# Interleaved RoPE on one core: a longer fp32 head on two queues, its result stored early, and longer VectorE steps

## Chip, cores, metric

The kernel runs on one core of a Trainium2 chip. The metric is the device time of one execution in microseconds (us), as a median over runs. Times inside an execution are counted from the start of the profile's span. The span of a profiled run is about 1.8 us shorter than its device time (before: 316.0 against 317.78). "The packet records" below are the trace's single DMA packets, with their start, length, queue and size.

## The reference

```python
# x: (8, 2048, 16, 64) fp32; cos, sin: (2048, 32) fp32
x_pairs = x.reshape(batch, seq_len, num_heads, head_dim // 2, 2)
x1, x2 = x_pairs[..., 0], x_pairs[..., 1]
out1 = x1 * cos - x2 * sin        # cos, sin broadcast over batch and heads
out2 = x1 * sin + x2 * cos
out = np.stack([out1, out2], axis=-1).reshape(batch, seq_len, num_heads, head_dim)
```

The input is 67.1 MB of fp32 and the output as much. There are three vector passes per element, and nothing for TensorE.

## The kernel before

Each of the 128 partitions holds 16 consecutive positions (`K = 16`) of each of the 8 batches, 1024 values a position. A batch is loaded by GpSimd's software queue, which casts fp32 to bf16 on the way, is rotated in place by VectorE in steps of `KP` positions, and is stored by the same queue, cast back to fp32. Five batch buffers (`NX = 5`) exist, so five loads are queued at once at the start, and load 5 needs the buffer that store 0 frees. Two small exceptions use fp32 and the SP queue, which does not cast: the first `HEAD = 2` positions of batch 0 come in early, and the last `TAIL = 4` positions of batch 7 go out from a buffer that ScalarE has cast.

```python
KP = 4; NX = 5; HEAD = 2; TAIL = 4
def load(b, k0=0):                       # ... allocate tiles[b], bf16
    nc.gpsimd.dma_start(out=tiles[b][:, k0:], in_=x_t[b, :, k0:])
def store(b, k1=K):
    nc.gpsimd.dma_start(out=out_t[b, :, :k1], in_=tiles[b][:, :k1])
def rotate(b, k0, k1):
    # ... three VectorE passes over positions k0..k1:
    # qt = xp * s_tab ; xp = xp * c_tab ; xp = xp + qt with each pair swapped

head = stage.tile([P, TAIL, HD], fp32, name="st")
for k in range(HEAD):
    nc.sync.dma_start(out=head[:, k : k + 1], in_=x_t[0, :, k : k + 1])
nc.sync.dma_start(out=cos_sb, in_=cos_t)
nc.sync.dma_start(out=sin_sb, in_=sin_t)
load(0, HEAD)
for b in range(1, NX):
    load(b)
nc.scalar.copy(out=tiles[0][:, :HEAD], in_=head[:, :HEAD])
# ... VectorE builds the bf16 tables s_tab, c_tab from sin_sb, cos_sb
for b in range(B):
    if b == 0:
        rotate(b, 0, HEAD)
        rotate(b, HEAD, KP)
    for k0 in range(KP if b == 0 else 0, K, KP):
        rotate(b, k0, k0 + KP)
    if b < B - 1:
        store(b)
    if b >= 1 and b - 1 + NX < B:
        load(b - 1 + NX)
store(B - 1, K - TAIL)
# ... ScalarE casts the last TAIL positions to fp32, the SP queue stores them
```

## Time and profile before

| | before |
|---|---|
| time, median of the runs beside the changed kernel | 317.45 us (317.34 to 317.79, 6 runs) |
| VectorE busy, first to last | 221.8 us, from 44.2 to 269 us |
| first packet to last packet of the DMA engines | 1.74 to 314.8 us |
| first and second store issued | 74.5 and 102.2 us |

From the page of the kernel before: the span, the busy times, the rows of 40 slices (tenths busy), the queues (packets, MB, share of the time of 16 engines) and the HBM traffic.

```profile
span 316.0 us, 198 instructions
...
DVE 221.8 (70%) x102; ACT 6.9 (2%) x4; POOL 8.9 (3%) x20
...
DVE  0000039999999999999999999999999999100000
...
DMA  9899999999999999999999999999999999999996
...
q0 software_dynamic: 2304, 98.04, 96.8%
q1 hardware_dynamic: 720, 3.67, 3.1%
...
HBM read 67.63 MB, written 67.11 MB: 426 GB/s over the span
```

VectorE (DVE) is idle for the first five slices and the last five, while the DMA row is at 9 throughout. The two queues' shares add up to the whole span. The Trainium skill ("DMA: Bandwidth & Descriptors", "Specifications") gives 435 GB/s as the ceiling of the fabric. The 426 GB/s over the whole span, start and end included, are 98% of that. A second limit on that page, about 358 GB/s of HBM per core (a stack's bandwidth divided by the two cores that share it), is not what this trace shows; here one core runs.

The timeline of the kernel before: start, duration, engine, line and operation, and in brackets the idle time ahead of it and what ended that. SPq is the issue of a DMA on the SP queue; a POOL line with `DMA_DIRECT2D` is an issue on the software queue.

```profile
0.74 0.85 SPq L85 DMA_DIRECT2D st<-in_x_dram  x2
1.24 2.80 POOL L56 DMA_DIRECT2D xt<-in_x_dram  x5 [0.80 <-PEq L144]
1.64 0.42 SPq L86 DMA_DIRECT2D cos_sb<-in_cos_dram  x1
2.11 0.43 SPq L87 DMA_DIRECT2D sin_sb<-in_sin_dram  x1
6.36 1.28 ACT L92 ACT_TABLE_LOAD   x1 [6.36 <-DMA st<-in_x_dram]
...
44.22 0.45 DVE L94 CAST s_tab<-sin_sb 128x512 bf16<-128x512 f32 x1 [44.22 <-DMA sin_sb<-in_sin_dram]
...
74.53 0.54 POOL L59 DMA_DIRECT2D out_dram<-xt  x1 [70.48 <-DVE xt L80]
...
102.17 0.54 POOL L59 DMA_DIRECT2D out_dram<-xt  x1 [27.11 <-DVE xt L80]
...
121.79 0.54 POOL L56 DMA_DIRECT2D xt<-in_x_dram  x1 [19.08 <-DMA out_dram<-xt]
```

Two things are to be seen. The sine table, 256 KB issued at 2.1 us, lands only at 44.2 us. And both first stores are queued before the engines need them. The trace's records of single packets show the last queued load ending at 101.8 us and the second store's data starting at 120.6 us, directly behind the first's. A packet of the software queue is one partition's 64 KB of fp32 and occupies an engine for 2.437 us (load) or 2.447 us (store).

### The profile page before, as it was taken

Reading aid. Unit: us, or ns where it says so; the run is one execution under the profiler, and the core shown is the slowest. Engines: PE = TensorE matmul, PEld = TensorE weight load, DVE = VectorE, ACT = ScalarE, POOL = GpSimd, SP = SyncE. Lnnn points to the kernel's source line nnn. Section 1 sums busy time; section 2 is a strip of 40 time slices with the busy share of each in tenths; the row PEclk is TensorE's granted clock in tenths of the full one; section 3 lists DMA queues with packets and bytes.
Section 4 is the critical chain, followed back from the end, with each engine's and each line's share of the span. In section 5 each row is a group of like instructions: output and inputs, shape, how many; then the busy total and the mean of one; then the engine's idle time right before and its main releaser. Section 6 shows DMA issues by size and latency. Waiting matters only on the chain.

```text
span 316.0 us, 198 instructions
## 1 busy us (share of the span) xinstructions
DVE 221.8 (70%) x102; ACT 6.9 (2%) x4; POOL 8.9 (3%) x20
## 2 busy tenths in 40 slices
DVE  0000039999999999999999999999999999100000
ACT  1200000000000000000000000000000000000400
POOL 3000000000000000000000000000000000000000
DMA  9899999999999999999999999999999999999996
GB/s 241 198 257 212 212 207 236 228 199 199 253 212 265 398 498 431 398 332 261 203 399 465 328 203 199 481 448 265 199 307 423 398 440 481 406 398 481 417 431 263
DMA packets 3025, 101.72 MB, mean 322 GB/s; under 512 B 336, under 2 KB 336, under 8 KB 848
## 3 DMA queue, kind: packets, MB, share of 16 engines
q0 software_dynamic: 2304, 98.04, 96.8%
q1 hardware_dynamic: 720, 3.67, 3.1%
q14 instruction: 1, 0.01, 0.0%
HBM read 67.63 MB, written 67.11 MB: 426 GB/s over the span
## 4 chain that ended last, share of the span: by engine, by line
another core or an unknown queue 91%; DMA 2%; ACTq 1%; ACT 1%; SPq 0%; issue 0%
DMA st<-in_x_dram 2%; ACTq L144 1%; ACT xt L92 1%; ACT L92 0%; SPq L85 0%; ACT xt L116 0%; ACTq L116 0%; ACTq L92 0%
## 5 line engine op out<-in xcount | busy, mean ns | idle before, releaser
L75 DVE TENSOR_TENSOR xt<-xt,c_tab 128x4096 bf16<-128x4096 bf16 (+1 forms) x33 | 73.5, 2228 | 1.1
L80 DVE TENSOR_TENSOR xt<-xt,qt 128x4096 bf16<-128x4096 bf16 (+1 forms) x33 | 73.5, 2228 | 1.1
L74 DVE TENSOR_TENSOR qt<-xt,s_tab 128x4096 bf16<-128x4096 bf16 (+1 forms) x33 | 73.5, 2228 | 1.1
L94 DVE CAST s_tab<-sin_sb 128x512 bf16<-128x512 f32 x1 | 0.5, 453 | 44.2 <-DMA sin_sb<-in_sin_dram 44.2
L59 POOL DMA_DIRECT2D out_dram<-xt x8 | 4.3, 535 | 202.1 <-DVE xt L80 202.1
L116 ACT COPY xt<-xt 1x1 bf16<-1x1 bf16 x1 | 0.2, 193 | 286.3 <-DMA out_dram<-xt 286.3
L56 POOL DMA_DIRECT2D xt<-in_x_dram x8 | 4.4, 561 | 52.1 <-DMA out_dram<-xt 51.3
L117 ACT CAST st<-xt 128x4096 f32<-128x4096 bf16 x1 | 3.6, 3599 | 0.0
L92 ACT CAST xt<-st 128x2048 bf16<-128x2048 f32 x1 | 1.9, 1899 | 0.0
L92 ACT ACT_TABLE_LOAD x1 | 1.3, 1283 | 6.4 <-DMA st<-in_x_dram 6.4
L96 DVE CAST c_tab<-cos_sb 128x1024 bf16<-128x1024 f32 x1 | 0.7, 684 | 0.0
L95 DVE TENSOR_SCALAR s_tab<-sin_sb 128x512 bf16<-128x512 f32 x1 | 0.4, 443 | 0.0
L133 POOL MEMSET const-float32-0.0<- 128x1 f32 x1 | 0.1, 99 | 0.2 <-issue 0.2
L133 POOL MEMSET const-bfloat16-1.0<- 128x1 bf16 x1 | 0.1, 102 | 0.0
L133 POOL MEMSET const-float32-1.0<- 128x1 f32 x1 | 0.1, 99 | 0.0
L133 POOL MEMSET const-uint8-127<- 128x1 uint8 x1 | 0.1, 99 | 0.0
## 6 DMA issues: line engine op xcount, KB each, us to landing
xt<-in_x_dram POOLq DMA_DIRECT2D x7, 4096.0 KB, 58.0
out_dram<-xt POOLq DMA_DIRECT2D x1, 6144.0 KB, 49.4
xt<-in_x_dram POOLq DMA_DIRECT2D x1, 3584.0 KB, 22.7
out_dram<-st SPq DMA_DIRECT2D x1, 2048.0 KB, 15.5
st<-in_x_dram SPq DMA_DIRECT2D x2, 512.0 KB, 4.5
cos_sb<-in_cos_dram SPq DMA_DIRECT2D x1, 256.0 KB, 22.4
sin_sb<-in_sin_dram SPq DMA_DIRECT2D x1, 256.0 KB, 42.1
out_dram<-xt POOLq DMA_DIRECT2D x7, 54.0
```

Of the source, the lines that this page charges most:

```text
L56: nc.gpsimd.dma_start(out=tiles[b][:, k0:], in_=x_t[b, :, k0:])
L59: nc.gpsimd.dma_start(out=out_t[b, :, :k1], in_=tiles[b][:, :k1])
L74: nc.vector.tensor_tensor(out=rows(qt[:, :nk]), in0=rows(xp), in1=tab(s_tab), op=mult)
L75: nc.vector.tensor_tensor(out=rows(xp), in0=rows(xp), in1=tab(c_tab), op=mult)
L80: nc.vector.tensor_tensor(out=x3, in0=x3, in1=q_swap, op=add)
L92: nc.scalar.copy(out=tiles[0][:, :HEAD], in_=head[:, :HEAD])
L94: nc.vector.tensor_copy(out=s2[:, :, 0], in_=sin_sb)
L95: nc.vector.tensor_scalar_mul(s2[:, :, 1], sin_sb, -1.0)
L96: nc.vector.tensor_copy(out=c_tab.rearrange("p k (i j) -> p (k i) j", j=2), in_=cos_sb.to_broadcast([P, K * D2, 2]),)
L117: nc.scalar.copy(out=tail, in_=tiles[B - 1][:, K - TAIL :])
L133: nc = _bacc.Bacc("TRN2", target_bir_lowering=False, num_devices=1)
L144: with _tile.TileContext(nc) as tc:
```

## The change

Its intent seems to be to start the vector work earlier and to use the engines better. Four head positions instead of two come in fp32, one DMA each, in turn on the SP and the Activation queue, and each queue brings one table. The rotated head goes back out early in fp32 on the SP queue. VectorE works in steps of 8 positions, which halves its instructions.

```diff
-    KP = 4
+    KP = 8
-    HEAD = 2
+    HEAD = 4
+    HEAD_RUNS = [(0, 1), (1, 2), (2, 4)]
...
-    def store(b, k1=K):
-        nc.gpsimd.dma_start(out=out_t[b, :, :k1], in_=tiles[b][:, :k1])
+    def store(b, k0=0, k1=K):
+        nc.gpsimd.dma_start(out=out_t[b, :, k0:k1], in_=tiles[b][:, k0:k1])
...
         for k in range(HEAD):
-            nc.sync.dma_start(out=head[:, k : k + 1], in_=x_t[0, :, k : k + 1])
+            q = (nc.sync, nc.scalar)[k % 2]
+            q.dma_start(out=head[:, k : k + 1], in_=x_t[0, :, k : k + 1])
         nc.sync.dma_start(out=cos_sb, in_=cos_t)
-        nc.sync.dma_start(out=sin_sb, in_=sin_t)
+        nc.scalar.dma_start(out=sin_sb, in_=sin_t)
...
                 rotate(b, 0, HEAD)
+                nc.scalar.copy(out=head, in_=tiles[b][:, :HEAD])
+                for k0, k1 in HEAD_RUNS:
+                    nc.sync.dma_start(out=out_t[b, :, k0:k1], in_=head[:, k0:k1])
                 rotate(b, HEAD, KP)
...
-                store(b)
+                store(b, HEAD if b == 0 else 0)
```

More of the change, by code (lines that the diff above doesn't have):

```diff
@@ L82 @@
     with tc.manual_schedule():
-        head = stage.tile([P, TAIL, HD], fp32, name="st")
+        head = stage.tile([P, HEAD, HD], fp32, name="st")
         for k in range(HEAD):
-            nc.sync.dma_start(out=head[:, k : k + 1], in_=x_t[0, :, k : k + 1])
+            q = (nc.sync, nc.scalar)[k % 2]
+            q.dma_start(out=head[:, k : k + 1], in_=x_t[0, :, k : k + 1])
         nc.sync.dma_start(out=cos_sb, in_=cos_t)
-        nc.sync.dma_start(out=sin_sb, in_=sin_t)
+        nc.scalar.dma_start(out=sin_sb, in_=sin_t)
         load(0, HEAD)
@@ L90 @@
             load(b)
-        nc.scalar.copy(out=tiles[0][:, :HEAD], in_=head[:, :HEAD])
+        nc.scalar.copy(out=tiles[0][:, :HEAD], in_=head)
         s2 = s_tab.rearrange("p k (i j) -> p (k i) j", j=2)
@@ L106 @@
             if b < B - 1:
-                store(b)
+                store(b, HEAD if b == 0 else 0)
             if b >= 1 and b - 1 + NX < B:
                 load(b - 1 + NX)
-        store(B - 1, K - TAIL)
+        store(B - 1, 0, K - TAIL)
         tail = stage.tile([P, TAIL, HD], fp32, name="st")
```

## The prediction

> **What bounds the kernel now.** The 16 DMA engines. The page's slice row shows DMA at 9 tenths or more in nearly all 40 slices (8 in the second, 6 in the last), VectorE 70% busy, ScalarE 2%. The queue part gives the software queue 96.8% and the hardware queue 3.1% of the engines' time. The trace's records of single packets sharpen this: from 4 to 312 us all 16 engines have a packet; only 0 to 4 us (first packet at 1.74, share 0.46) and 312 to 316 us (share 0.52) are not full. VectorE starts at 44.2 us, when the sine table lands (view of waits), ends at 269 and never stops for a load. The timeline shows the first store issued at 74.5 us, the second at 102, while the five loads queued at the start keep the engines busy until about 101. No idle DMA time is there to fill.
>
> A packet costs by its fp32 side, either way: load of 64 KB 2.437 us, store of 64 KB 2.447, 56 KB 2.129, 48 KB 1.84, 16 KB 0.611, 4 KB 0.159 (0.165 with the gap after it), table row of 2 KB 0.096.
>
> **The change, costed.**
> - Head: 2 MB instead of 1 in fp32 rows of 4 KB. Per engine 16 more packets x 0.165 = 2.6 us; the first cast load shrinks from 56 to 48 KB: 8 x 0.29 = 2.3. Net +0.3 us.
> - Early result: 16 packets of 4 KB and 8 of 8 KB (estimate 16 x 0.165 + 8 x 0.31 = 5.1 us); first store 48 instead of 64 KB: 8 x 0.6 = 4.8. Net +0.3 us.
> - Two issuing queues: an issue takes 0.42 us. First data can't come before 1.74 us; overlapped slow first packets (0.5 to 1 us) may return 0.2 to 0.5. The Trainium skill ("DMA: Bandwidth & Descriptors", "Issuing engines are not separate DMA queues") says queues share the 16 engines and save issue time only; the trace agrees so far as one queue fills all 16.
> - VectorE by 8: a pass takes 1.25 us for 2048 elements, 2.33 for 4096, so 0.17 fixed; 48 fewer save 8 us of VectorE, none on the critical path.
> - ScalarE: one more 3.6 us cast, off the path.
>
> **When compute starts.** The same page ("Queues, rings and completion order") has engines take turns between queues by packet. The trace agrees: cos landed 22.4 us after issue, its 8 packets per engine each behind a 2.13 us packet of the first load; sin behind the second load. After the change the last two head pieces either stay early or go behind the first load, so the tables land near 24 or near 44 us. I lean to 44 (0.6). Either way the first two stores are queued before 101 and 120 us, so the engines don't run dry.
>
> **Predicted time.** +0.6 us of packets, -0.3 at the start: 317.6 us; 8 in 10 within 316.2 to 318.8. Faster by over 2%: 0.02; within 2%: 0.96; slower: 0.02.
>
> **What would show it.** DMA slices at 9 throughout; hardware queue's share near 6%, software's near 94%; VectorE busy near 214 us; first store of tile 0 before 75 us; tail unchanged: last cast near 296 us, last store issued near 300.
>
> **What would make it wrong.** Small fp32 stores between loads costing far more than 0.16 us, or overlapping them in an engine (read of one with write of the other); tables landing after 65 us, so that the engines run dry; VectorE's longer passes holding up GpSimd's descriptors; a larger spread of the engines' ends.

## The result and the profile after

The changed kernel takes 318.09 us (317.87 to 318.12, 6 runs) against 317.45 us of before. Ratios in this document are the mean time of one kernel's fast runs over that of the other's of the same rounds, so they are not quite the ratio of the quoted medians. Here the ratio is 1.0017, 95% interval 1.0004 to 1.003: the same within 2%, and probably half a microsecond slower.

The same lines of the page of the changed kernel:

```profile
span 316.1 us, 165 instructions
...
DVE 214.2 (68%) x54; ACT 12.3 (4%) x5; POOL 8.9 (3%) x20
...
DVE  0000049999999999999999999999949994000000
...
DMA  9899999999999999999999999999999999999995
...
q0 software_dynamic: 2304, 95.42, 94.4%
q1 hardware_dynamic: 1008, 5.51, 5.6%
q10 hardware_dynamic: 432, 1.31, 1.1%
...
HBM read 67.63 MB, written 67.11 MB: 426 GB/s over the span
```

VectorE lost 7.6 us of work and the DMA row did not move. Work went from the software queue q0 to the hardware queues q1 (SP) and q10 (Activation), and the DMA engines stayed full. (The shares now add up to 101.1%. The completion records of the third early store are logged at 3.5 us each, 1.1% of the span, beside data packets that fill the engines by themselves; they are not time lost.) VectorE's row has a new hole at the thirtieth slice. The view of waits shows what it is: VectorE, now faster, catches up with the last load and waits for it.

```profile
DVE qt L77 <- DMA xt<-in_x_dram: 4.7, 1, 4.7
```

The timeline of the changed kernel, the same events:

```profile
0.74 0.89 ACTq L89 DMA_DIRECT2D st<-in_x_dram  x2
0.74 0.86 SPq L89 DMA_DIRECT2D st<-in_x_dram  x2
1.25 2.80 POOL L59 DMA_DIRECT2D xt<-in_x_dram  x5 [0.80 <-PEq L151]
1.65 0.42 SPq L90 DMA_DIRECT2D cos_sb<-in_cos_dram  x1
1.66 0.45 ACTq L91 DMA_DIRECT2D sin_sb<-in_sin_dram  x1
23.11 1.28 ACT L96 ACT_TABLE_LOAD   x1 [23.11 <-DMA st<-in_x_dram]
...
43.73 0.46 DVE L98 CAST s_tab<-sin_sb 128x512 bf16<-128x512 f32 x1 [43.73 <-DMA sin_sb<-in_sin_dram]
...
72.60 0.54 POOL L62 DMA_DIRECT2D out_dram<-xt  x1 [68.55 <-DVE xt L83]
...
99.36 0.54 POOL L62 DMA_DIRECT2D out_dram<-xt  x1 [26.22 <-DVE xt L83]
...
122.33 0.54 POOL L59 DMA_DIRECT2D xt<-in_x_dram  x1 [22.43 <-DMA out_dram<-xt]
```

The head is complete at 23.1 instead of 6.4 us, VectorE starts at 43.7 instead of 44.2 us, and the stores are queued 2 to 3 us earlier. None of this reaches the end, because in neither kernel did the engines wait for it. Load 5, which needs store 0 to have landed, goes out at 122.3 against 121.8 us.

### The profile page after: what moved, and what is told of

The parts are those of the page before. It is cut to its first block, busy times and chain, and to the rows that moved or that the text cites. A ratio compares the mean times of both kernels' runs of the same rounds, so it can differ in the third digit from the quotient of the medians.

```text
span 316.1 us, 165 instructions
## 1 busy us (share of the span) xinstructions
DVE 214.2 (68%) x54; ACT 12.3 (4%) x5; POOL 8.9 (3%) x20
## 3 DMA queue, kind: packets, MB, share of 16 engines
q0 software_dynamic: 2304, 95.42, 94.4%
## 4 chain that ended last, share of the span: by engine, by line
another core or an unknown queue 76%; DMA 13%; DVE 2%; ACT 2%; ACTq 0%; issue 0%
DMA sin_sb<-in_sin_dram 13%; ACT st L107 1%; ACT st L124 1%; DVE xt L78 1%; DVE xt L83 1%; DVE qt L77 1%; ACTq L89 0%; DVE s_tab L98 0%; DVE s_tab L99 0%; DVE c_tab L100 0%; ACTq L123 0%; ACT xt L123 0%; ACTq L124 0%; ACTq L107 0%
## 5 line engine op out<-in xcount | busy, mean ns | idle before, releaser
L77 DVE TENSOR_TENSOR qt<-xt,s_tab 128x8192 bf16<-128x8192 bf16 (+1 forms) x17 | 71.0, 4174 | 5.2 <-DMA xt<-in_x_dram 4.7
L78 DVE TENSOR_TENSOR xt<-xt,c_tab 128x8192 bf16<-128x8192 bf16 (+1 forms) x17 | 71.0, 4175 | 0.6
L83 DVE TENSOR_TENSOR xt<-xt,qt 128x8192 bf16<-128x8192 bf16 (+1 forms) x17 | 71.0, 4174 | 0.6
L98 DVE CAST s_tab<-sin_sb 128x512 bf16<-128x512 f32 x1 | 0.5, 457 | 43.7 <-DMA sin_sb<-in_sin_dram 43.7
L59 POOL DMA_DIRECT2D xt<-in_x_dram x8 | 4.4, 561 | 64.2 <-DMA out_dram<-xt 63.4
L107 ACT CAST st<-xt 128x4096 f32<-128x4096 bf16 x1 | 3.6, 3606 | 24.0 <-DVE xt L83 24.0
L124 ACT CAST st<-xt 128x4096 f32<-128x4096 bf16 x1 | 3.6, 3605 | 0.0
L96 ACT CAST xt<-st 128x4096 bf16<-128x4096 f32 x1 | 3.6, 3604 | 0.0
L96 ACT ACT_TABLE_LOAD x1 | 1.3, 1283 | 23.1 <-DMA st<-in_x_dram 23.1
```

The source lines that it names most:

```text
L77: nc.vector.tensor_tensor(out=rows(qt[:, :nk]), in0=rows(xp), in1=tab(s_tab), op=mult)
L78: nc.vector.tensor_tensor(out=rows(xp), in0=rows(xp), in1=tab(c_tab), op=mult)
L83: nc.vector.tensor_tensor(out=x3, in0=x3, in1=q_swap, op=add)
L96: nc.scalar.copy(out=tiles[0][:, :HEAD], in_=head)
L98: nc.vector.tensor_copy(out=s2[:, :, 0], in_=sin_sb)
L107: nc.scalar.copy(out=head, in_=tiles[b][:, :HEAD])
```

## Experiments

All but one run gave the right result. "Theory A" is the prediction's: 16 full DMA engines bound the kernel. "Rival B" is that VectorE's chain, which starts late, bounds it.

### One part of the change at a time, on the kernel before

**Steps of 8 (e1).** Only `KP = 4` became `KP = 8`.

> The kernel before, with only VectorE's steps of 8 positions instead of 4. Theory A (16 full DMA engines bound the kernel): VectorE busy falls from 222 to about 214 us, the time stays within 0.3 us. Rival B (VectorE's chain, from 44 us on, bounds): 5 to 8 us less.

Measured: 317.57 us against 317.47, ratio 1.0002 (0.999 to 1.0014). VectorE's busy time fell to 214.2 us, and it waited 4.2 us for a load. Rival B fails: 7.6 us of VectorE are worth nothing here.

**Two queues (e2).**

```diff
-            nc.sync.dma_start(out=head[:, k : k + 1], in_=x_t[0, :, k : k + 1])
+            q = (nc.sync, nc.scalar)[k % 2]
+            q.dma_start(out=head[:, k : k + 1], in_=x_t[0, :, k : k + 1])
...
-        nc.sync.dma_start(out=sin_sb, in_=sin_t)
+        nc.scalar.dma_start(out=sin_sb, in_=sin_t)
```

> The kernel before, with only its second head piece and its sine table issued on the Activation queue. Theory A (16 full DMA engines; the time is the sum of the packets' times): same packets, so within 0.5 us of before, at most 0.2 to 0.5 us less from the cold start; tables still at about 44 us or earlier, without effect. Rival C (a second hardware queue costs setup or turn-taking of its own): 0.3 us or more above before.

Measured: 317.44 us against 317.45, ratio 1.0 (0.9987 to 1.0013). From this kernel's waits, timeline and slices:

```profile
DVE s_tab L95 <- DMA sin_sb<-in_sin_dram: 24.1, 1, 24.1
```
```profile
54.40 0.54 POOL L59 DMA_DIRECT2D out_dram<-xt  x1 [50.36 <-DVE xt L80]
```
```profile
DVE  0009999999999999999999995799708996000000
...
DMA  9999999999999999999999999999999999999997
```

VectorE started 20 us earlier and queued the first store 20 us earlier, and the time did not move. The gained time came back as holes in VectorE's row, where it waits for loads. This is the clearest refutation of Rival B. Neither the cold-start gain nor Rival C's cost of a second queue shows.

**A head of 4 on the SP queue alone (e3).** `HEAD = 2` became `HEAD = 4`, with the empty call `rotate(b, HEAD, KP)` skipped.

> The kernel before, with only its fp32 head doubled to 4 positions, all on the SP queue. Theory A: 16 more packets of 4 KB per engine (0.165 us each with the gap), the first cast load 8 x 0.29 us less: +0.3 us (0.1 to 0.5). Rival B (VectorE's chain from its start at 44 us bounds the kernel): follows the tables, which now come a load later or not, so by up to 20 us more if the sine table lands near 64 us.

Measured: 338.35 us against 317.45, ratio 1.0658 (1.0644 to 1.0673). My +0.3 us was wrong by a factor of 70. Slices and timeline of this kernel:

```profile
DVE  0000000001999999999999999999999999995000
...
DMA  8999999999980595298989899898989898989997
```
```profile
82.98 0.45 DVE L94 CAST s_tab<-sin_sb 128x512 bf16<-128x512 f32 x1 [82.98 <-DMA sin_sb<-in_sin_dram]
...
112.70 0.54 POOL L59 DMA_DIRECT2D out_dram<-xt  x1 [108.66 <-DVE xt L80]
...
140.35 0.54 POOL L59 DMA_DIRECT2D out_dram<-xt  x1 [27.11 <-DVE xt L80]
```

The DMA row has two holes, at the 13th to 14th and the 16th to 17th slice. The table issued at 3.3 us landed at 83 us, VectorE began there, and the first store was queued at 112.7 us, 11 us after the loads had run out. The second came at 140.35 us, 7 us after the first had been written. Engine time lost in both, from the packet records: 12.5 + 8.3 = 20.8 us, which is the whole loss of 20.9 us. My words "follows the tables" under Rival B described the mechanism that took over; it belongs to Theory A with a condition, and I call that A2 below: the engines are full as long as stores are queued in time.

**Early fp32 store of the 2-position head (e4).** ScalarE casts the rotated head, two SP DMAs store it, and the first cast store begins at position 2.

> The kernel before, with only an early fp32 store of its 2 head positions (1 MB in rows of 4 KB on the SP queue). Theory A: 16 packets of 4 KB stored (0.172 us in the changed kernel's trace) against 8 x 0.31 us less in the first cast store: +0.3 us (0.1 to 0.6). Rival D (stores placed between loads overlap with them in an engine): at least 1 us less than before, since 1 MB is 2.4 us of the 16 engines.

Measured: 317.49 us against 317.45, ratio 1.0001 (0.9987 to 1.0015). Rival D fails: stores between loads do not overlap with them by any amount worth having.

### Rows of 16 KB in the changed kernel (e5)

```diff
-    HEAD_RUNS = [(0, 1), (1, 2), (2, 4)]
+    HEAD_RUNS = [(0, 4)]
...
-        for k in range(HEAD):
-            q = (nc.sync, nc.scalar)[k % 2]
-            q.dma_start(out=head[:, k : k + 1], in_=x_t[0, :, k : k + 1])
+        nc.sync.dma_start(out=head, in_=x_t[0, :, :HEAD])
```

> The changed kernel, with its 2 MB head as one DMA in rows of 16 KB each way instead of 4 KB and 8 KB rows. Theory A, with the packets' fixed cost as the whole of the change's loss: 16 KB take 0.611 us instead of 4 x 0.165 to 4 x 0.172, so 8 x 0.05 us less on the load and about 0.3 us less on the store: back to the kernel before within 0.3 us. If it stays 0.6 us over before, the loss is not the size of the rows.

Measured: 317.66 us, ratio to before 1.0006 (0.9993 to 1.0018). That is the outcome foreseen, but not for the reason foreseen: summed from the packet records, its packets take 315.49 us an engine, no less than the changed kernel's 315.33. Its profile lacks a delay of 0.4 us that the changed kernel has after its last packet (see "Why the prediction was right"). The intervals of e5 and of the changed kernel overlap as well, so nothing here shows that small rows cost the half microsecond.

### Moving VectorE's work without changing the packets

**Tables first (e6).** Both table DMAs were put ahead of the two head pieces on SP.

> The kernel before, with both tables issued ahead of the two head pieces on the same SP queue: same packets in another order. VectorE should start near 10 us instead of 44 and issue the first store near 50 us instead of 74. Theory A: time within 0.4 us of before; the loads queued at the start still hold the engines until about 101 us. Rival B: 20 to 30 us less.

Measured: 318.62 us (317.25 to 319.44, 6 runs) against 317.47, ratio 1.0028 (1.0007 to 1.0049). The prediction of when VectorE starts was wrong: it built its tables at 4.2 us, but then stood until 49.2 us, because now the second head piece landed only at 46.0 us. The first store was queued at 78.3 us. So it is not the tables that are slow; whatever stands third and fourth on that queue is. Since the passes started later than before, and not earlier, this run does not test Rival B. The time scattered over 2.2 us, and four of the six runs lie outside the 0.4 us that I expected. In the profiled run the first load's packets took 2.21 us on average against 2.13 before, and up to 3.46 us; why is open. At its end the 16 engines finish (completion records of the last store) at 314.10 us on average against 314.07 before, but the last of them at 315.65 against 314.80: the extra time is a wider spread of the engines' ends, and not more work.

**Steps of 2 (e7) and of 1 (e8).** `KP = 2` and `KP = 1`, with the special case for batch 0 dropped.

> The kernel before, with VectorE's steps of 2 positions: VectorE busy about 1.23 us x 192 + 1.6 = 238 us, done near 285 us instead of 269. The last cast store's turn comes near 294 us, so Theory A: within 0.5 us of before. Rival B: about 16 us more.

> The kernel before, with VectorE's steps of 1 position: fixed part of 0.17 us paid 384 times, VectorE busy about 0.7 x 384 = 270 us (estimate), done near 315 us. That is past 294 us, where the last cast store's turn comes, so the slack is used up and the engines run dry before the end: both theories expect more time, Theory A about 15 to 25 us more (end of VectorE, then the last 8 MB stored, part of it already overlapped), Rival B about 45 us more. DMA slices below 9 before the end would show it.

Measured: e7 318.31 us, ratio 1.0024 (1.0011 to 1.0037), with VectorE busy 236.6 us, 15 us more than before. This is 0.8 us over before, outside the half microsecond that I expected and far from 16. In the profiled runs the extra is again a spread: the engines finish at 314.07 us on average in both, the last at 315.37 against 314.80. e8 took 339.58 us, ratio 1.0694 (1.0678 to 1.0709), +22 us and so within Theory A's 15 to 25, with VectorE busy 267.1 us; its DMA row:

```profile
DMA  9999899999999999999999999999999850595688
```

So VectorE could give away 15 us (e7) without the engines running dry. With 45 us (e8) they do, here at the end instead of at the start.

### What the second queue does (e12, e10, e11)

**The changed kernel with everything on SP (e12).**

```diff
-            q = (nc.sync, nc.scalar)[k % 2]
-            q.dma_start(out=head[:, k : k + 1], in_=x_t[0, :, k : k + 1])
+            nc.sync.dma_start(out=head[:, k : k + 1], in_=x_t[0, :, k : k + 1])
...
-        nc.scalar.dma_start(out=sin_sb, in_=sin_t)
+        nc.sync.dma_start(out=sin_sb, in_=sin_t)
```

> The changed kernel with one part undone: all four head pieces and both tables on the SP queue. Theory A2 (engines full unless VectorE starts so late that the first stores miss the end of the queued loads near 101 us; on one queue every piece beyond the first two lands one cast load later, so the sine table lands near 83 us): first store near 112 us, second near 139 us, engines dry about 20 us in two gaps, time 335 to 338 us, the early fp32 store filling part of the gap but not moving the second store. Rival A (packets alone): within 0.5 us of the changed kernel's 318.1.

Measured: 337.24 us against 317.53, ratio 1.0621 (1.0605 to 1.0637). First two stores and the DMA row:

```profile
111.92 0.54 POOL L62 DMA_DIRECT2D out_dram<-xt  x1 [107.88 <-DVE xt L83]
...
138.68 0.54 POOL L62 DMA_DIRECT2D out_dram<-xt  x1 [26.22 <-DVE xt L83]
```
```profile
DMA  8999999999985690589899898989898989898996
```

A2 holds to within the stated microseconds. Within the change, the second queue is worth 19 us (337.24 against 318.09; runs of the kernel before agree within 0.1 us), although on the kernel before (e2) it was worth nothing.

**e3 with its tables on the Activation queue (e10).** Only the two table DMAs went from SP to Activation.

> The slow run with the head of 4 on SP (338.35 us), with only its two tables moved to the Activation queue. Theory A2 (the late sine table is the whole loss): tables land within some us, VectorE then waits for the last head piece near 43 us and its cast, starts its passes near 49 us, first store near 78 us, time back at 317.3 to 318.3 us. Rival (the four head pieces themselves cost it): stays above 325 us.

Measured: 317.42 us, ratio 0.9997 (0.998 to 1.0013): the 21 us are gone. The sine table and the first two stores:

```profile
18.35 0.45 DVE L94 CAST s_tab<-sin_sb 128x512 bf16<-128x512 f32 x1 [18.35 <-DMA sin_sb<-in_sin_dram]
...
87.13 0.54 POOL L59 DMA_DIRECT2D out_dram<-xt  x1 [83.09 <-DVE xt L80]
...
114.78 0.54 POOL L59 DMA_DIRECT2D out_dram<-xt  x1 [27.11 <-DVE xt L80]
```

The way there was not quite as expected: the sine table landed at 18.4 us and the last head piece at 53.7 instead of 43 us, so the first store came at 87.1 us. That is still before 101 us, and the second, at 114.8 us, before the first had landed (121.6 us). Four head pieces in fp32 cost nothing measurable by themselves.

**A head of 3 on SP (e11).** `HEAD = 3` on the kernel before.

> The kernel before, with a head of 3 positions on SP: a dose between 2 (317.45 us) and 4 (338.35 us). Theory A2: sine table near 63 us, first store near 92 us and so in time, second near 120 us against the end of the first store's data near 119 to 120 us, so a gap of 0 to 4 us: 317.5 to 321.5 us. If the loss went evenly with the landing of the table it would be about 328 us.

Measured: 319.44 us against 317.53, ratio 1.006 (1.0045 to 1.0075), +1.9 us. Its wait for the table and the second store:

```profile
DVE s_tab L94 <- DMA sin_sb<-in_sin_dram: 63.4, 1, 63.4
```
```profile
121.39 0.54 POOL L59 DMA_DIRECT2D out_dram<-xt  x1 [27.11 <-DVE xt L80]
```

A table 19 us later cost 1.9 us, the next 20 us cost 19 more: a threshold and not a slope.

The packet records give one figure that accounts for the losses to within a microsecond: when the second store's first packet starts.

| | sine table lands | second store issued | its first packet | later than before by | time, over before of the same rounds |
|---|---|---|---|---|---|
| before | 44.2 | 102.2 | 120.6 | | |
| after | 43.7 | 99.4 | 120.3 | -0.3 | +0.6 |
| e11 | 63.4 | 121.4 | 122.5 | +1.9 | +1.9 |
| e12 | 83.0 | 138.7 | 139.8 | +19.2 | +19.7 |
| e3 | 83.0 | 140.4 | 141.5 | +20.9 | +20.9 |

(Microseconds. "Over before" is the difference of the medians. In the rows of after and e12, 0.4 us of it come after the last packet; see below.)

**Bytes alone (e9).** The changed kernel without the three early stores: `HEAD_RUNS[:0]`. The result is wrong, 2.1 MB of it are never written.

> The changed kernel without its early fp32 store, so that 2 MB of the result are never written: wrong on purpose, to measure what bytes alone are worth. Theory A: 16 packets of 4 KB at 0.172 and 8 of 8 KB at 0.333 us less per engine, 5.2 to 5.5 us less than the changed kernel: 312.5 to 313.2 us. Rival B (VectorE's chain bounds): no change.

Measured: 312.9 us, ratio to before 0.9853 (0.9838 to 0.9867). That is 5.2 us below the changed kernel's 318.09 (runs of the kernel before agree within 0.1 us). Of these, 4.8 us are packets (310.52 us an engine against 315.33), and 0.4 us the changed kernel's delay after the last packet, which e9 lacks. 2.1 MB in 4.8 us are about 436 GB/s, near the 426 GB/s of the whole span.

No correct run beats both kernels beyond its interval. The lowest correct one, e10 at 317.42 us, can't be told from before. That is what full engines leave: of the 316 us of the span, only about 2 us at the start and 2 at the end are not packets.

## Why the prediction was right

The time, 317.6 us within 316.2 to 318.8, came out at 318.09. Point by point:

- **"What bounds the kernel now. The 16 DMA engines."** Shown. VectorE was made 7.6 us faster (e1), started 20 us earlier (e2) and made 15 us slower (e7), and the time moved by at most 0.8 us; 2 MB less traffic gave 5.2 us (e9), 4.8 of them by its packets. The bound holds on a condition that e3, e8, e11 and e12 show: stores must be queued in time.
- **"48 fewer save 8 us of VectorE, none on the critical path."** Shown: 7.6 us saved, 4.2 to 4.7 of them spent waiting for the last load.
- **Tables near 24 or near 44 us, lean to 44.** They landed at 43.7, each queue's third DMA behind the second load.
- **What would show it.** Hardware queues 6.7% against "near 6%", software 94.4%, VectorE 214.2 us, first store at 72.6 us, last cast at 295.7 us, last store issued at 299.4 us. All as said (1.1 of the 6.7% are the overlong completion records).
- **"+0.6 us of packets, -0.3 at the start."** The measured difference of the medians is +0.64 us, inside the range, but the terms were not right, so that the small sum came near is luck. Summed from the packet records without completion records, packets take 315.33 us an engine against 315.15 (neighbouring records overlap a little, so this exceeds the 313.1 us from first to last packet): +0.2 and not +0.6 us. No start gain shows: the first packet starts at 1.75 against 1.74 us, and e2 gained nothing.
- **A term that the prediction lacked.** In the trace's records of SP's instructions, SP waits at the end of the kernel for one DMA semaphore (the counter that a DMA raises when it has landed) after another. In the kernel before, the last store's semaphore is in the last of these waits (7th of 7). In the changed kernel and in e12 the last store uses again the semaphore of an earlier DMA, which is in the 3rd of 9: SP passes it at 314.85 us and the last one, long satisfied, at 315.22. From the last store's landing to the end of the span it is 1.26 us in the changed kernel, 1.25 in e12, and 0.86 to 0.89 in the other twelve traces. So about 0.4 of the 0.64 us come after the last packet. No run was made to test this alone; the rest, some 0.2 us, is open.
- **The mis-sized term: "Two issuing queues ... may return 0.2 to 0.5."** and, next to it, "Head: ... Net +0.3 us." I costed each part alone and added. Alone, two queues are worth 0.0 (e2), a longer head costs 20.9 (e3), and both together cost next to nothing (e10, the changed kernel). I had the turn-taking in the section on when compute starts, and "tables landing after 65 us, so that the engines run dry" in the list of dangers, but I did not see that the second queue is what keeps the longer head from that.

The step that was incomplete is the sentence "The trace agrees so far as one queue fills all 16". One queue does fill the engines. What a second queue adds is not bandwidth but turns. On the SP queue of e3, the packet records show the six DMAs ending at 4.2, 5.9, 21.7, 42.3, 62.4 and 82.4 us: two run ahead of the software queue, whose first packet starts at 5.0 us, then one passes per 20 us load, since each of its small packets waits for one 2.4 us packet of the load. In the changed kernel SP's three end at 4.9, 18.3 and 38.4 us, and Activation's at 5.2, 20.7 and 41.0 us: two pass per load, one from each queue.

## What to carry to other kernels

When the DMA engines are full from end to end, ask of each change only whether it alters the packets' total or makes the engines run dry; here idle or slow compute cost nothing until a store came too late. Find that deadline in the trace (here the second store's issue at about 119.5 us: its data's start before, 120.6, less the 1.1 us that e3 and e11 show from issue to first packet) and check every change against it. Small transfers queued beside large ones paid here by turns and not by bytes, so put the ones that compute waits for first, or on a queue of their own, and cost the parts of a change together. For differences under a microsecond, look also at what follows the last packet and at how far apart the engines end.

## What the Trainium skill lacked or had wrong

- "DMA: Bandwidth & Descriptors", "Issuing engines are not separate DMA queues", says that starting DMAs on several engines saves only the time to initiate them. For bandwidth the runs agree (e2: 317.44 against 317.45 us). For latency they don't: with four head pieces and two tables the second queue was worth 19 us (337.24 against 318.09 us), because each queue gets its own turns beside a busy software queue.
- The same page, "SWDGE vs HWDGE vs iDMA", puts a packet at preferably 4096 B or less. Here the casting DMAs' packets, as the trace records them, held up to 64 KB of fp32 and took 2.44 us, so one turn was that long and a 256 KB sine table took 42 us (before) to 80 us (e3) from issue to landing. The page's "Queues, rings and completion order", which gives the turn-taking by packet, agrees with the order seen, but does not say that about two hardware-queue DMAs run ahead of five large loads issued in the same microseconds (e3: data complete at 4.2 and 5.9 us, then 21.7, 42.3, 62.4 and 82.4).
- The same page, "Where 436 GB/s comes from", derives the ceiling from the SBUF ports. Here a packet cost the same by its fp32 side in HBM, 64 KB in 2.437 us (load) or 2.447 us (store), though the bf16 side in SBUF carries half the bytes; 16 engines at that pace are 430 GB/s of fp32, and the last store, fp32 on both sides, took 0.611 us for 16 KB, which is 429 GB/s. So a cast to bf16 on the way saved no DMA time, which the page doesn't say. Its note that about 358 GB/s of HBM binds such transfers did not hold for this one core: 426 GB/s. (The page's own "Bandwidth" part has 425 measured on a single core and keeps about 358 for both cores streaming; the note leaves that condition out.)
- No page gives this chip's price of mixing: 1 MB of fp32 stores in 4 KB rows, put between casting loads, left the time where it was (e4: ratio 1.0001).
